# A transformer trunk's opening stage rearranged: transfers in stages behind X, five parts' modulation as column-tiled products, seven product chains side by side and the eighth at the end

## The chip, the cores and the metric

The kernel runs on one core of one Trainium2 chip. TensorE (PE) multiplies matrices into PSUM, VectorE (DVE) and ScalarE (ACT) work on tiles in SBUF and PSUM, GpSimd (POOL) and SyncE (SP) mostly issue transfers. The metric is the device time of one execution in microseconds; less is better.

## The reference

Two layers over 256 latent tokens (x) and 256 context tokens (ctx), width 1024. This is cut to what the opening stage computes:

```python
def rms_norm(x, g):
    y = xf * lax.rsqrt(jnp.mean(xf * xf, axis=-1, keepdims=True) + EPS)
    return (y * g).astype(x.dtype)
def modulate(x, g, shift, scale):
    return rms_norm(x, g) * (1 + scale) + shift
def swiglu(h, w13, w2):
    a, b = jnp.split(h @ w13, 2, axis=-1)
    return (jax.nn.silu(a) * b) @ w2
def half_ffn(x, g, shift, scale, gate, w13, w2):
    return x + 0.5 * gate * swiglu(modulate(x, g, shift, scale), w13, w2)
...
    silu_c = jax.nn.silu(c); silu_cc = jax.nn.silu(c_ctx)
    for i in range(DEPTH):                       # DEPTH = 2
        m  = (silu_c @ w_mod[i] + b_mod[i]).reshape(b, 1, N_MOD, d)     # N_MOD = 9
        mc = (silu_cc @ w_mod[i] + b_mod[i]).reshape(1, 1, N_MOD, d)
        cs = half_ffn(cs, norm_g[i, 0], mc[:, :, 0], mc[:, :, 1], mc[:, :, 2], ffn_w13[i, 0], ffn_w2[i, 0])
        x  = half_ffn(x, norm_g[i, 0], m[:, :, 0], m[:, :, 1], m[:, :, 2], ffn_w13[i, 0], ffn_w2[i, 0])
        # then attention + pooling (layer 0) or a gated MLP (layer 1), then a second half_ffn
```

So before the first product of the first `w13`, the kernel needs the reciprocal root of the mean square of x and ctx, and shift and scale of the first modulation, which are products of a vector (SiLU of c, and of c_ctx) with `w_mod`.

## The kernel before

The tokens lie transposed: X is 8 parts (index k) of 128 channels by 512 columns (256 latent, 256 context). A product in full precision is split in three fp32r matmuls by `mm3`: weights and activations are each held as a rounded high part and the rest (`whi`/`wlo` or `sh`/`sl` for weights, AH/AL for activations), made by `split` (a cast on ScalarE, L153, and a subtraction on VectorE, L154). The first feed-forward has 22 tiles f of a pair of outputs; `start` computes the first four (f = 0 to 3, so 8 chains of products in 8 PSUM banks, 8 parts each, 3 matmuls each: 192 products), and `ffn` goes on with f = 4 and takes these four from `started`. `ffn` loads weights with `load_w`.

What `start` does, in order:

- It loads c, the identity, X and a few rows of `w_mod`; c is spread over the partitions (L665 on TensorE, L667 on ScalarE) into `cc`.
- Squares of X (L679) are summed over the partitions by matmuls with ones (L680); root (L681) and reciprocal (L685) give `rb`.
- The modulation comes in two ways. By dot products on VectorE: `use_mod` multiplies a row tile `wm` with `cc` and sums (L80); a part takes two tiles for two streams, so four of these; `finish_mod` adds the bias (L92, `mod`) and forms the scale (L98, `gs`). By rows on TensorE: `by_rows` multiplies c with `wn` tiles (L697, 384 columns for the 3 last parts), copies the two rows out (L701) and turns them with small matmuls (L704). Before, parts 0 to 4 go by dot products and parts 5 to 7 by rows, in one block.
- Eight steps (i) take the parts in `order`. A step splits the part's weights `raw`, forms `xr` = X times rb (L721), `h` by scale and shift in two halves (L724), AH and AL, and then issues its 24 products.

Engines work each in its own queue, strictly in order; a scheduler in the tile framework has set that order when the program was built, except where an instruction is pinned (`tc.keep_in_program_order`). Transfers are issued by SP (waits of one hold up all behind it), and in `run_mods` by GpSimd. Buffers of a name rotate (`bufs`): `sq` has 2, `raw4` 2, `raw` 2, `whi` and `wlo` 3, `wm` 4, PSUM banks 8.

Of the kernel before, what the change touches and what calls it, by code (L numbers as in the profile page):

```python
# [25 lines left out]
NR = 3  # L26
# [9 lines left out]
def trunk(ctx: ExitStack, tc: tile.TileContext, I, out):  # L36
# [47 lines left out]
    def finish_mod(layer, j, n=1, ks=slice(0, NK)):  # L84
# [7 lines left out]
        V.tensor_tensor(out=m, in0=m, in1=b.broadcast_to([P, ns, n, nk]), op=ALU.add)  # L92
# [32 lines left out]
    def load_w(src, n, pin=lambda ins: ins):  # L125
        raw = wpool.tile([P, 2048], F32, name="raw", bufs=2)
        hi = wpool.tile([P, 2048], F32R, name="whi", bufs=3)
        lo = wpool.tile([P, 2048], F32R, name="wlo", bufs=3)
        nc.sync.dma_start(out=raw[:, :n], in_=src)
        for c in (slice(0, n // 2), slice(n // 2, n)):  # L130
            split(hi[:, c], lo[:, c], raw[:, c], pin)
        return hi, lo
# [82 lines left out]
    def ffn(fi, layer, sub, n, mods, after, started=()):  # L215

        defer = n == T
        with tc.tile_pool(name=f"ffn{fi}", bufs=1) as fp:
            HH = fp.tile([P, NH, 2 * T], F32R, name="HH")
            HL = fp.tile([P, NH, 2 * T], F32R, name="HL")  # L220
            for half in range(2):
                hc = half * T if n == T else 0
                for fl in range(NH):
# [3 lines left out]
                    else:  # L227
                        hi, lo = load_w(I["w13"][fi, f], 2048)
# [410 lines left out]
    def start():  # L639
        ng = 4  # L640
        order = (0, 5, 1, 6, 2, 7, 3, 4)
        with tc.tile_pool(name="start", bufs=1) as sp:
            def get_raw(k):
                raw = sp.tile([P, ng, 2 * P], F32, name="raw4", bufs=2)
                nc.sync.dma_start(out=raw, in_=I["w13"][0, 0:ng, :, k * 2 * P:(k + 1) * 2 * P]
                                  .rearrange("f p c -> p f c"))
                return raw

            cT = sp.tile([P, 2, NK], F32, name="cT")
            nc.sync.dma_start(out=cT, in_=I["cT"])  # L650
            nc.sync.dma_start(out=ident, in_=I["ident"])
            wm = {(0, 0): load_mod(0, 0, nc.sync)}
            for k in range(0, NK, 2):
                nc.sync.dma_start(out=X[:, k:k + 2], in_=I["xc"][:, k:k + 2])
            wm[0, 1] = load_mod(0, 1, nc.sync)
            S.activation(out=cT, in_=cT, func=AF.Silu)

            S.activation(out=rb[:, 0:1], in_=cT[:, 0, 0:1], func=AF.Sqrt, scale=0.0, bias=epsb)

            for st in range(2):  # L660
                for h in range(2):
                    ps = bank()
                    for k4 in range(4):
                        k = 4 * h + k4
                        PE.matmul(ps[:, k4 * P:k4 * P + P], cT[:, st, k:k + 1].broadcast_to([P, P]),  # L665
                                  ident, start=True, stop=True)
                    S.copy(cc[:, st, h * 512:h * 512 + 512], ps)  # L667
            nc.sync.dma_start(out=par, in_=I["par"])
            wn = [wpool.tile([P, 2, 2 * NR * P], F32, name=n, bufs=3 if i > 1 else 2)
                  for i, n in enumerate(("raw", "raw", "whi", "wlo"))]  # L670
            for i in range(4):
                nc.sync.dma_start(out=wn[i], in_=I["w_modr"][:, 2 * i:2 * i + 2])
            raws = {0: get_raw(0)}
            wm.update({(1, h): load_mod(0, 2 + h, nc.sync) for h in range(2)})
            raws[order[1]] = get_raw(order[1])
            ps = bank()
            for k in range(NK):
                sq = tmp.tile([P, 2 * T], F32, name="sq", bufs=2)
                S.activation(out=sq, in_=X[:, k], func=AF.Square)  # L679
                PE.matmul(ps, ones, sq, start=k == 0, stop=k == NK - 1)  # L680
            S.activation(out=rb, in_=ps, func=AF.Sqrt, scale=1.0 / D, bias=epsb)  # L681
            for h in range(2):
                use_mod(0, h, wm[0, h])
            finish_mod(0, 0, 2, slice(0, 1))
            V.reciprocal(rb, rb)  # L685
            sh = sp.tile([P, NK, ng - 2, 2 * P], F32R, name="sh")
            sl = sp.tile([P, NK, ng - 2, 2 * P], F32R, name="sl")
            wh, wl = ([wpool.tile([P, NK, 2 * P], F32R, name=n, bufs=3) for _ in range(2)]
                      for n in ("whi", "wlo"))

            def by_rows():

                row = sp.tile([2, 2 * NR * P], F32, name="row")
                ps = [bank() for _ in range(2)]
                for k in range(NK):
                    for j in range(2):
                        PE.matmul(ps[j][0:2, :NR * P], cT[:, :, k],  # L697
                                  wn[k // 2][:, k % 2, j * NR * P:(j + 1) * NR * P],
                                  start=k == 0, stop=k == NK - 1)
                for j in range(2):  # L700
                    S.copy(row[:, j * NR * P:(j + 1) * NR * P], ps[j][0:2, :NR * P])  # L701
                ps = bank()
                for i in range(2 * NR):
                    PE.matmul(ps[:, 2 * i:2 * i + 2], row[:, i * P:i * P + P], ident[0:2, 0:2],  # L704
                              start=True, stop=True)
                for st in range(2):
                    V.tensor_copy(mod[:, st, :16].rearrange("p (j k) -> p j k", j=2)[:, :, NK - NR:],
                                  ps[:, 0:4 * NR].rearrange("p (j k s) -> p s j k", j=2, k=NR)[:, st])
                finish_mod(0, 0, 2, slice(NK - NR, NK))

            by_rows()
# [127 lines left out]
```

## Time and profile before

| | |
|---|---|
| median of 3 runs | 1141.98 us (1141.77 to 1142.43) |
| profiled execution | 1142.17 us, of which the span of instructions is 1140.4 us |
| TensorE busy | 1132.2 us (99%) |
| VectorE, ScalarE busy | 863.6 us (76%), 522.0 us (46%) |
| transfers | 242.72 MB, mean 213 GB/s |
| granted TensorE clock | 1.000 |

A profile names a group of instructions by line, engine, operation and tiles (output<-inputs). Matmuls overlap: a record's duration holds the time until its result stands, and the distance between starts is the rate. An fp32 matmul leaves two records, an fp32r one leaves one. Span times count from the first instruction.

### The profile page before, as it was taken

The page shows a single profiled execution, that of the slowest core. Times are in us where ns is not written, and L with a number is a line of the kernel's source. Part 1 is how long each engine was busy: PE and PEld are TensorE (multiplying, and loading weights), DVE is VectorE, ACT ScalarE, POOL GpSimd, SP SyncE. Part 2 cuts the span into 40 slices and gives each one's busy share as a digit, 9 for nine tenths or more (in the row PEclk, how much of TensorE's full clock was granted, in tenths as well). Part 3 has the DMA queues.
Part 4 walks back from the last instruction along what each step waited for, and adds up shares of the span by engine and source line. Part 5 has one row for each costly group of instructions (what it writes and reads, how often), then busy time and mean ns, then how long its engine had stood idle before and what let it go on. Part 6 is the DMA issues. An engine that isn't in the chain of part 4 may idle for free.

```text
span 1140.4 us, 19165 instructions
## 1 busy us (share of the span) xinstructions
PE 1132.2 (99%) x7696; PEld 1033.9 (91%) x7696; DVE 863.6 (76%) x1582; ACT 522.0 (46%) x816; POOL 68.4 (6%) x140
## 2 busy tenths in 40 slices
PE   8999999999999999999999999999999999999998
PEld 4888888888888897899999999999999899999998
DVE  5967787878789979777778887656667788756663
ACT  5552212223223357664335456435445866434442
POOL 0000111122222200000000000000000000000000
PEclk9999999999999999999999999999999999999999
DMA  8844656788888850556687566456447536546543
GB/s 323 310 148 156 197 186 234 279 282 325 294 297 306 305 196 11 222 172 223 212 305 264 187 219 218 161 167 219 174 143 257 185 114 219 176 154 237 178 143 114
DMA packets 52408, 242.72 MB, mean 213 GB/s; under 512 B 5600, under 2 KB 11488, under 8 KB 38880
## 3 DMA queue, kind: packets, MB, share of 16 engines
q1 hardware_dynamic: 33888, 174.39, 43.4%
q0 software_dynamic: 18432, 67.12, 17.4%
q8 instruction: 60, 0.98, 0.4%
q14 instruction: 28, 0.23, 0.1%
HBM read 240.44 MB, written 1.05 MB: 212 GB/s over the span
## 4 chain that ended last, share of the span: by engine, by line
PE 97%; DVE 1%; ACT 1%; DMA 1%; issue 0%; SPq 0%; DVEq 0%; ACTq 0%
PE ps L148 30%; PE ps L149 30%; PE ps L150 30%; PE ps L697 1%; PE ps L618 1%; PE ps L619 1%; PE ps L617 1%; PE ps L680 1%; PE ps L665 1%; DMA raw<-in_w_out_a 0%; ACT whi L153 0%; PE ps L501 0%; PE ps L469 0%; DVE st L473 0%; PE ps L172 0%; ACT pe L477 0%
## 5 line engine op out<-in xcount | busy, mean ns | idle before, releaser
L148 PE MATMUL ps<-AH,wlo 128*128 128x258 f32 (+2 forms) x1664 | 507.1, 305 | 0.3 <-ACT AH L153 0.3
L149 PE MATMUL ps<-AH,whi 128*128 128x258 f32 (+2 forms) x1664 | 506.6, 305 | 0.0
L150 PE MATMUL ps<-AL,whi 128*128 128x258 f32 (+2 forms) x1664 | 505.5, 305 | 0.0
L153 ACT CAST whi<-raw 128x1024 fp32r<-128x1024 f32 (+2 forms) x354 | 313.7, 921 | 363.7 <-PE ps L150 260.3
L154 DVE TENSOR_TENSOR wlo<-raw,whi 128x1024 fp32r<-128x1024 f32 (+2 forms) x354 | 367.6, 1064 | 54.4 <-ACT whi L153 53.4
L148 PEld LDWEIGHTS ps<-AH,wlo 128*128 128x128 f32 x1664 | 316.3, 190 | 16.1 <-issue 1.1
L149 PEld LDWEIGHTS ps<-AH,whi 128*128 128x128 f32 x1664 | 314.3, 189 | 14.7 <-issue 0.5
L150 PEld LDWEIGHTS ps<-AL,whi 128*128 128x128 f32 x1664 | 313.4, 189 | 14.5 <-issue 0.2
L150 PE MATMUL ps<-HL,whi 128*128 128x256 f32 (+1 forms) x704 | 218.0, 310 | 0.0
L149 PE MATMUL ps<-HH,whi 128*128 128x256 f32 (+1 forms) x704 | 218.0, 310 | 0.0
L148 PE MATMUL ps<-HH,wlo 128*128 128x256 f32 (+1 forms) x704 | 218.0, 310 | 0.0
L80 DVE CUSTOM_DVE_ANT_0 wm<-wm,cc 128x1024 f32<-128x1024 f32 x138 | 164.7, 1219 | 6.1 <-DMA wm<-in_w_mod 5.0
L148 PEld LDWEIGHTS ps<-HH,wlo 128*128 128x128 f32 x704 | 132.5, 188 | 7.8
L150 PEld LDWEIGHTS ps<-HL,whi 128*128 128x128 f32 x704 | 132.5, 188 | 7.7
L149 PEld LDWEIGHTS ps<-HH,whi 128*128 128x128 f32 x704 | 132.6, 188 | 7.7
L72 POOL DMA_DIRECT2D wm<-in_w_mod x128 | 67.7, 529 | 546.2 <-DVE mod L80 508.6
L206 ACT ACTIVATE sa<-sa,cb 128x256 f32<-128x256 f32 x66 | 33.6, 510 | 119.7 <-DVE sa L205 116.4
L246 DVE SCALAR_TENSOR_TENSOR X<-ps,gate,X 128x256 f32<-128x256 f32 x64 | 30.9, 482 | 48.0 <-PE ps L150 47.9
L204 DVE COPY cb<-ps 128x1 f32<-128x1 f32 x66 | 10.3, 155 | 72.8 <-PE ps L150 72.7
L212 DVE TENSOR_TENSOR h<-ps,sa 128x512 f32<-128x512 f32 x22 | 15.2, 692 | 43.4 <-PE ps L150 34.2
L80 DVE CUSTOM_DVE_ANT_0 junk<-wm,cc 128x1024 bf16<-128x1024 f32 x34 | 41.4, 1218 | 8.6 <-ACT cc L667 7.2
L154 DVE TENSOR_TENSOR HL<-h,HH 128x256 fp32r<-128x256 f32 (+1 forms) x88 | 42.3, 485 | 0.0
(162 smaller groups left out, 705.3 us busy)
## 6 DMA issues: line engine op xcount, KB each, us to landing
raw<-in_w SPq DMA_DIRECT2D x84, 1024.0 KB, 4.9
wm<-in_w_mod POOLq DMA_DIRECT2D x128, 512.0 KB, 5.0
raw<-in_w SPq DMA_DIRECT2D x64, 704.0 KB, 4.1
wm<-in_w_mod SPq DMA_DIRECT2D x10, 512.0 KB, 6.4
raw<-in_w_in_a SPq DMA_DIRECT2D x5, 1024.0 KB, 7.8
raw<-in_w SPq DMA_DIRECT2D x8, 512.0 KB, 5.3
raw<-in_w_out_a SPq DMA_DIRECT2D x4, 1024.0 KB, 5.0
raw<-in_w_in_cu SPq DMA_DIRECT2D x4, 1024.0 KB, 4.8
```

Source lines behind the costliest of these rows:

```text
L72: eng.dma_start(out=w, in_=I["w_mod"][layer, i])
L80: pin(V.tensor_tensor_reduce(out=res, in0=w, in1=cc[:, st, :], scale=1.0, scalar=0.0, op0=ALU.mult, op1=ALU.add, accum_out=mod[:, 2 * laye ...
L148: PE.matmul(ps, wl, xh, start=first, stop=False)
L149: PE.matmul(ps, wh, xh, start=False, stop=False)
L150: PE.matmul(ps, wh, xl, start=False, stop=last)
L153: S.copy(hi, src)
L154: pin(V.tensor_tensor(out=lo, in0=src, in1=hi.bitcast(F32), op=ALU.subtract))
L206: S.activation(out=sa[:, :T], in_=sa[:, :T], func=AF.Silu, bias=cb[:, 0:1])
L212: V.tensor_tensor(out=h32[:, :n], in0=ps[1][:, :n], in1=sa[:, :n], op=ALU.mult)
L246: V.scalar_tensor_tensor(out=X[:, m, :T], in0=ps[:, :T], scalar=gate[:, 2 * layer, sub, m:m + 1], in1=X[:, m, :T], op0=ALU.mult, op1=ALU.add)
L617: PE.matmul(ps[b], AL[:, k, ts], hi[:, ws], start=(k == 0), stop=False)
L618: PE.matmul(ps[b], AH[:, k, ts], hi[:, ws], start=False, stop=False)
```

## The change

- **Transfers.** SP issues c with a selector (`cs`), the identity, X in five pieces, par, the rows of part 3 and the weights of part 3. The rows and weights of part 4, two `wm` tiles and the weights of part 0 are issued by ScalarE's queue (`late`), behind the root. All of these are pinned; the first tiles' weights in `ffn` are pinned too. `raw4` has three buffers.
- **Broadcast of c.** VectorE forms diagonal blocks of the identity times c, and four matmuls with ones spread them; VectorE copies them to `cc`.
- **Sums.** Squares of parts 0 to 5 are added in pairs on VectorE before the matmul with ones; parts 6 and 7 go alone. Three filler matmuls (`warm`) stand between them.
- **Rows.** Parts 3 to 7 now go by rows, one part at a time, 8 matmuls each with 32 columns of weights (c in `c32`, zeros beside it), placed in four column groups of 32; then one copy and two turns with the selector, which also adds the four groups. Part 3's row product stands before the stage; those of parts 4, 5, 6, 7 stand between products of the step before their own. Parts 0, 1, 2 go by dot products, placed in steps 2, 3 and 5 (`jobs`, i = 1, 2, 4).
- **Chains.** Seven chains take each part as it comes, in the order 3, 4, 0, 5, 1, 6, 2, 7; the eighth (f = 3, second output) runs over all parts at the end. The first step runs in two halves of 256 columns, and its AH is written directly.

The diff, cut to its core:

```diff
-    def load_w(src, n, pin=lambda ins: ins):
+    def load_w(src, n, pin=lambda ins: ins, dma_pin=lambda ins: ins):
...
-        order = (0, 5, 1, 6, 2, 7, 3, 4)
+        order = (3, 4, 0, 5, 1, 6, 2, 7)
+        jobs = {1: 0, 2: 1, 4: 2}
...
-                raw = sp.tile([P, ng, 2 * P], F32, name="raw4", bufs=2)
+                raw = sp.tile([P, ng, 2 * P], F32, name="raw4", bufs=3)
...
+            sync, late = InOrder(nc.sync), InOrder(S)
+            sync.dma_start(out=cs, in_=I["cs"])
+            sync.dma_start(out=ident, in_=I["ident"])
+            for ks in (slice(0, 2), slice(2, 4), slice(4, 6), slice(6, 7), slice(7, 8)):
+                sync.dma_start(out=X[:, ks], in_=I["xc"][:, ks])
+            sync.dma_start(out=par, in_=I["par"])
+            get_rows(3)
+            raws[3] = get_raw(3)
...
             for st in range(2):
+                V.tensor_tensor(out=diag[:, st], in0=ident.unsqueeze(1).broadcast_to([P, NK, P]),
+                                in1=c32[:, :, st:st + 1].broadcast_to([P, NK, P]), op=ALU.mult)
                 for h in range(2):
-                    ps = bank()
-                    for k4 in range(4):
-                        k = 4 * h + k4
-                        PE.matmul(ps[:, k4 * P:k4 * P + P], cT[:, st, k:k + 1].broadcast_to([P, P]),
-                                  ident, start=True, stop=True)
-                    S.copy(cc[:, st, h * 512:h * 512 + 512], ps)
+                    PE.matmul(bc[2 * st + h], ones, diag[:, st, 4 * h:4 * h + 4],
+                              start=True, stop=True)
...
                 S.activation(out=sq, in_=X[:, k], func=AF.Square)
-                PE.matmul(ps, ones, sq, start=k == 0, stop=k == NK - 1)
+                if k in (0, 2, 4):
+                    even = sq
+                    continue
+                if k < 6:
+                    V.tensor_tensor(out=sq, in0=even, in1=sq, op=ALU.add)
+                PE.matmul(ps, ones, sq, start=k == 1, stop=k == NK - 1)
+                if k < 6:
+                    warm(1, rw)
...
+            get_rows(4, eng=late)
+            raws[4] = get_raw(4, late)
+            wm.update({(0, j): load_mod(0, j, late) for j in range(2)})
+            raws[0] = get_raw(0, late)
...
+            def by_rows(k):
+                w = rows.pop(k)
+                for kt in range(NK):
+                    g = kt % 4
+                    pin(PE.matmul(rw[32 * g:32 * g + 32, :2 * P], c32[:, kt], w[:, kt],
+                                  start=kt < 4, stop=kt >= 4))
+                row = sp.tile([P, 2 * P], F32, name="row", bufs=2)
+                pin(S.copy(row, rw[:, :2 * P]))
+                for j in range(2):
+                    PE.matmul(rw[:, 2 * P + 2 * j:2 * P + 2 * j + 2], row[:, j * P:j * P + P], sel,
+                              start=True, stop=True)
+                finish_mod(0, 0, 2, slice(k, k + 1), ...)
...
+            by_rows(order[0])
+            warm(4, ps)
-            pss = [[bank(), bank()] for _ in range(ng)]
+            pss = [[bank() for _ in range(2 if f < ng - 1 else 1)] for f in range(ng)]
...
+                if i == 0:
+                    for ts in halves:
+                        if ts.start:
+                            pin(V.reciprocal(rb[:, ts], rb[:, ts]))
+                            subs(pin)
+                            rest(halves[0])
+                        pin(V.tensor_tensor(out=xr[:, ts], in0=X[:, k, ts], in1=rb[:, ts], op=ALU.mult))
+                        if ts.start == 0:
+                            casts(pin)
+                        normed(ts, AH[:, k, ts])
+                        normed(ts, h[:, ts])
+                    rest(halves[1])
...
+                if i in jobs:
+                    d = jobs[i]
+                    for j in range(2):
+                        use_mod(0, 2 * d + j, wm.pop((d, j)), tc.keep_in_program_order)
+                    finish_mod(0, 0, 2, slice(d, d + 1))
...
+                else:
+                    for f, ab in todo:
+                        if ahead is not None and (f, ab) == (1, 0):
+                            by_rows(ahead)
+                        mm3(pss[f][ab], *tile(f, ab), AH[:, k, :2 * T], AL[:, k, :2 * T], False,
+                            i == NK - 1)
+            ps = bank()
+            for k in range(NK):
+                mm3(ps, *tile(ng - 1, 1, k), AH[:, k, :2 * T], AL[:, k, :2 * T], k == 0, k == NK - 1)
```

Three places in the queues as built. TensorE's queue at the front, before (sums L680, row products L697, turns L704, first products):

```order
L665 MATMUL ps<-ident,cT 128x128 x16
L680 MATMUL ps<-sq,ones 128x512 x8
L697 MATMUL ps<-raw,cT 2x384 x8
L697 MATMUL ps<-whi,cT 2x384 x4
L697 MATMUL ps<-wlo,cT 2x384 x4
L704 MATMUL ps<-ident,row 128x2 x3
L148 MATMUL ps<-AH,sl 128x512
```

And now, from the last sums to the second half of the first step (L713 sums, L736 row products, L741 turns, L703 fillers, L832 products of 256 columns):

```order
L713 MATMUL ps<-sq,ones 128x512 x2
L736 MATMUL ps<-raw,c_99 32x256 x8
L741 MATMUL ps<-cs,row 128x2 x2
L703 MATMUL ps<-X,ones 128x256 x4
L832 MATMUL ps<-AH,sh 128x256 x4
L832 MATMUL ps<-AH,whi 128x256 x3
L832 MATMUL ps<-AL,sh 128x256 x4
L832 MATMUL ps<-AL,whi 128x256 x3
L832 MATMUL ps<-AH,sl 128x256 x4
L832 MATMUL ps<-AH,wlo 128x256 x3
L736 MATMUL ps<-raw,c_99 32x256 x8
L832 MATMUL ps<-AH,sh 128x256 x4
```

One row product of 8 narrow matmuls stands where 16 stood, and the next one stands between the two halves of the first step.

ScalarE's queue behind the last square, before (L681 the root, L724 h, L153 casts, L701 the copy of the rows):

```order
L681 ACTIVATE rb<-ps,epsb 128x512 [waits PE_49]
L724 ACTIVATE h_227<-sa,mod,gs 128x256 [waits DVE_49]
L724 ACTIVATE h_227<-sa,mod,gs 128x256
L153 CAST AH<-h_227 128x512 [waits Activation_49]
L153 CAST sh<-raw_131 128x512 [waits DMAHW5_49]
L153 CAST whi<-raw_131 128x256 x2
L701 COPY row<-ps 2x384 [waits PE_49] x2
```

And now (L720 the root in halves, L667 transfers, L739 the copy of part 3's row, L767 casts of its weights, L775 AH and h):

```order
L720 ACTIVATE rb<-ps,epsb 128x256 [waits PE_49]
L720 ACTIVATE rb<-ps,epsb 128x256
L667 DMA raw<-in_w_modr 128x2048
L667 DMA raw_150<-in_w 128x4x256
L667 DMA wm<-in_w_mod 128x1024 x2
L667 DMA raw_156<-in_w 128x4x256
L739 COPY row<-ps 128x256 [waits PE_49]
L767 CAST sh<-raw_97 128x512 [waits DMAHW1_49]
L767 CAST whi<-raw_97 128x256 x2
L775 ACTIVATE AH<-sa,mod,gs 128x256 [waits DVE_49]
```

Five transfers stand between the root and the copy of the first row.

VectorE's queue in the stage, before (L80 dot products, with buffer numbers), around the second step:

```order
L80 ISA junk_234,mod_76<-wm_135,cc_68 128x1024
L80 ISA mod_76 128x1
L92 TENSOR_TENSOR mod_76<-mod_76,par_69 128x2x2x3
L154 TENSOR_TENSOR sl_175<-raw4_137,sh_174 128x512
L98 SCALAR_TENSOR_TENSOR gs_77<-mod_76,par_69 128x2x3
L80 ISA wm_135,mod_76<-wm_135,cc_68 128x1024
L80 ISA mod_76 128x1
L154 TENSOR_TENSOR wlo_178<-raw4_137,whi_176 128x256
L92 TENSOR_TENSOR mod_76<-mod_76,par_69 128x2x2
```

And now, from part 4's AL (second step) to part 0's scale (third step; L81 dot products, L93 and L100 as L92 and L98):

```order
L156 TENSOR_TENSOR AL_73<-h32_273,AH_72 128x512
L81 ISA junk_288,mod_76<-wm_152,cc_68 128x1024
L81 ISA mod_76 128x1
L81 ISA wm_152,mod_76<-wm_152,cc_68 128x1024
L81 ISA mod_76 128x1
L81 ISA junk_291,mod_76<-wm_154,cc_68 128x1024
L81 ISA mod_76 128x1
L81 ISA wm_154,mod_76<-wm_154,cc_68 128x1024
L81 ISA mod_76 128x1
L93 TENSOR_TENSOR mod_76<-mod_76,par_69 128x2x2
L100 SCALAR_TENSOR_TENSOR gs_77<-mod_76,par_69 128x2
```

Part 0's four dot products stand between the second step's last operation and the third step's scale.

176 lines of the change are left out of this document (100 added, 76 removed).

## Prediction

> **What bounds the kernel now.** I read the page first (busy shares, the chain that ended last), then TensorE's waits, then the timeline of the first 30 us engine by engine, then stretches of the opening stage.
>
> ```profile
> span 1140.4 us, 19165 instructions
> PE 1132.2 (99%) x7696; PEld 1033.9 (91%) x7696; DVE 863.6 (76%) x1582; ACT 522.0 (46%) x816; POOL 68.4 (6%) x140
> ...
> PE 97%; DVE 1%; ACT 1%; DMA 1%; issue 0%; SPq 0%; DVEq 0%; ACTq 0%
> ```
>
> TensorE is 97% of the chain that ended last. Its waits are short, and the largest is the very first:
>
> ```profile
> PE ps L665 <- DMA ident<-in_ident: 3.3, 1, 3.3
> PE ps L501 <- ACT pt L493: 0.9, 2, 0.5
> ```
>
> So the end moves only if TensorE gets less work, or waits. The work that is not products of the model sits at the front:
>
> ```profile
> 3.31 6.15 PE L665 MATMUL ps<-ident,cT 128*128 128x128 f32 x32 [3.31 <-DMA ident<-in_ident]
> 9.30 7.42 PE L680 MATMUL ps<-sq,ones 128*128 128x512 f32 x16
> 16.65 5.32 PE L697 MATMUL ps<-raw,cT 128*2 128x384 f32 x16
> ...
> 27.06 0.82 PE L704 MATMUL ps<-ident,row 2*128 2x2 f32 x6
> 27.82 0.50 PE L148 MATMUL ps<-AH,sl 128*128 128x512 f32 x1
> ...
> 28.71 0.82 PE L704 MATMUL ps<-ident,row 2*128 2x2 f32 x6
> ...
> 34.42 0.40 PE L148 MATMUL ps<-AH,sl 128*128 128x512 f32 x1
> 67.76 0.39 PE L148 MATMUL ps<-AH,sl 128*128 128x512 f32 x1
> ```
>
> Columns are start, duration. The first of the 192 opening products starts at 27.82. Steps 2 and 8 of the stage begin at 34.42 and 67.76; 144 products lie between, so one takes 33.34/144 = 0.2315 us and a step of 24 takes 5.56. The stage therefore ends at 67.76 + 5.56 = 73.3. Inside it TensorE never stops, though VectorE is full as well:
>
> ```profile
> 34.00:64.00 30.00, 30.00 (x131) 24.35 (x130) 30.00 (x61) 18.49 (x36) 2.24 (x4) 1.00 0.83 281
> ```
>
> (length, TensorE busy, weight loads, then VectorE's 30.00 and ScalarE's 18.49.) The question is thus one number: when the changed kernel has done the same 192 products, against 73.3. What follows the stage is the same work.
>
> **Prices.** The 16 row products of 384 columns (L697) fill 16.65 to 27.06, 0.65 each; by columns, a plain fp32 matmul of 512 takes 0.87 and one of 256 takes 0.43. Two records make one such matmul. The other prices:
>
> ```profile
> L679 ACT ACTIVATE sq<-X 128x512 f32<-128x512 f32 x8 | 4.9, 628 | 2.3 <-PE ps L680 1.7 <-DMA X<-in_xc 0.6
> L154 DVE TENSOR_TENSOR AL<-h,AH 128x512 fp32r<-128x512 f32 x8 | 5.5, 687 | 0.0
> L154 DVE TENSOR_TENSOR wlo<-raw,whi 128x256 fp32r<-128x256 f32 x16 | 6.3, 418 | 0.0
> L154 DVE TENSOR_TENSOR wlo<-raw,whi 128x1024 fp32r<-128x1024 f32 x3 | 3.6, 1219 | 0.1
> L153 ACT CAST AH<-h 128x512 fp32r<-128x512 f32 x8 | 5.0, 620 | 0.2
> L153 ACT CAST whi<-raw 128x1024 fp32r<-128x1024 f32 x3 | 3.1, 1038 | 0.0
> L724 ACT ACTIVATE h<-sa,mod,gs 128x256 f32<-128x256 f32 x16 | 8.9, 595 | 9.4 <-DVE sa L721 6.8 <-DVE gs L98 2.4
> L685 DVE RECIPROCAL rb<-rb 128x512 f32<-128x512 f32 x1 | 3.4, 3352 | 1.8 <-ACT rb L681 1.8
> L701 ACT COPY row<-ps 2x384 f32<-2x384 f32 x2 | 0.9, 468 | 2.2 <-PE ps L697 2.2
> ```
>
> ```profile
> 16.76 0.69 ACT L681 ACTIVATE rb<-ps,epsb 128x512 f32<-128x512 f32 x1 [1.22 <-PE ps L680]
> ```
>
> ```profile
> 25.25 1.22 DVE L80 CUSTOM_DVE_ANT_0 junk<-wm,cc 128x1024 bf16<-128x1024 f32 x1
> ...
> 26.51 1.23 DVE L80 CUSTOM_DVE_ANT_0 wm<-wm,cc 128x1024 f32<-128x1024 f32 x1
> ...
> 30.86 0.17 DVE L92 TENSOR_TENSOR mod<-mod,par 128x12 f32<-128x12 f32 x1
> ...
> 31.55 0.16 DVE L98 SCALAR_TENSOR_TENSOR gs<-mod,par 128x6 f32<-128x6 f32 x1
> ```
>
> A dot product on VectorE (L80) costs 1.25 with its read-out, and a part by dot products takes four, 5.0.
>
> **Part one: up to the first product.** The broadcast of c becomes four matmuls of 512 behind a VectorE product of 128x1024 (1.22, as L154 at that size). With the identity there at 3.31, TensorE starts at 4.53. It starts slowly:
>
> ```profile
> 3.50:8.00 4.50, 4.50 (x22) 1.00 0.96 350
> 8.40:9.20 0.80, 0.80 (x10) 1.00 0.97 348
> ```
>
> The same L665 records come every 0.21 us until about 8.2 and every 0.1 after, although the granted clock (1.00) reads full in both; full speed came 4.9 us after the first matmul. Taking the same 4.9 here, it comes at 9.4: 2.45 of the 3.48 us of broadcast are done by then, and they end at 10.45. (Bounds: full speed at 8.2 gives 9.8; none before they end gives 11.5.)
>
> Then the sums of squares. They are one matmul for a pair, but only two sq buffers remain, so the second square of a pair waits for TensorE to have read the pair before: matmul 0.87 and some 0.16 until its result stands (a product's record is 0.39 long at 0.2315 apart), square 0.63, addition 0.69, handoffs 0.1, in all 2.45 a round. Two rounds bring the third pair to 15.35; it, a filler and the last two sums (0.87 + 0.43 + 0.87 + 0.87 + 0.16) end at 18.55. Before, the root started at 16.76: what is removed here in matmuls is lost to a ring of waits. The root of one half (0.6) ends at 19.2 and its reciprocal (half of 3.35) at 20.9.
>
> ScalarE now issues five transfers between the roots and the copy of the first row. Such an issue stands on SP alone:
>
> ```profile
> 2.11 1.91 SPq L654 DMA_DIRECT2D X<-in_xc  x4
> ```
>
> 0.48 each, so 2.4 from about 19.0 to 21.4. (Bounds: nothing, if the queue runs on; the row copy is then ready at 19.6, and the reciprocal sets the pace, 1.6 earlier.) The copy of part 3's row, behind them, ends at 21.9, two transposes (of three in 0.82) at 22.45, mod and gs (0.17 + 0.16 and handoffs) at 22.9, the half xr (0.35) at 23.25, AH (0.60) at 23.9. Four filler matmuls (1.73) behind the transposes end at 24.1. The first product starts at 24.1, 3.7 us before 27.82.
>
> **Part two: row products inside the stage.** Before, all 10.4 us of L697 and one block of transposes lay ahead of 27.82, one block after. Now the rows of parts 4 to 7 run between products. Concurrency of column groups shows in the attention:
>
> ```profile
> 446.77 1.09 PE L492 MATMUL ps<-ident,sa 128*128 128x128 f32 x8
> 447.80 0.65 PE L501 MATMUL ps<-pt,VV 128*64 128x256 f32 x2
> 448.81 1.73 PE L501 MATMUL ps<-pt,VV 128*64 128x256 f32 x13 [0.37 <-ACT pt L493]
> ```
>
> Thirteen records of 256 columns in 1.73, the last 0.38 long: 0.1125 apart, where whole-width ones take 0.215. Two groups of 64 columns overlap almost fully. Four groups of 32 I take as four at once: 16 records by 0.054, 0.86, with some 0.1 for each change of mode (the first L501 starts 0.2 behind the last L492 record where 0.11 is usual), 1.05. Ends: pairs only, 1.9; none, 3.5. The Trainium skill, "TensorEngine Tiling (Array Packing)", Theoretical Speedup, allows up to four times for 32 columns, and "TensorE: Matmul & The Clock Gate", Part 3, gives 2.38 times measured for three column tiles; by that efficiency (an estimate) four would take about 1.1 instead of 0.86, and the sum would be 0.9 longer. L501's 1.9 of 2 stands nearer to full overlap. With two transposes (0.45), each row product costs 1.5 on TensorE, four 6.0.
>
> The first step in halves is 42 products of 256: 0.12 each, as
>
> ```profile
> 500.00:550.00 50.00, 50.00 (x416) 1.00 0.58 200
> ```
>
> (all of 258 columns) shows, 5.05 against 4.85: +0.2. The eighth chain is moved, not added.
>
> **Part three: the new waits.** In the queues as they now stand:
> - Step 1, first half: VectorE does xr, the other half's reciprocal (1.68), three subtractions (1.3 pipelined) and only then AL: 26.6. TensorE has finished its seven AH products at 24.95: wait 1.65. The half ends at 28.3, row product 29.35, second half and transposes 32.35.
> - Step 2 (part 4): row copy 30.0, transposes 30.5, gs 30.9, two h (1.09), AH (0.62), 32.7: wait 0.35. It lasts 21 x 0.2315 = 4.86, to 37.55.
> - Step 3 (part 0): four dot products stand behind part 4's AL (33.4): 38.4, gs 38.8, h 39.9, AH 40.55. Wait 3.0. This is the largest.
> - Step 4 (part 5): step 3 with a row product ends at 46.9, but part 5's gs stands behind four more dot products (from 41.2): gs 46.5, h and AH 48.35. Wait 1.5.
> - Steps 5 to 8: VectorE has two dot-product parts behind it and stays ahead. No wait. The weights of the next tile (two casts of 1.04, subtraction 1.22) fit behind the eighth chain's 5.56.
>
> Together 6.5. Dropping two of five dot-product parts from VectorE costs or gains nothing beyond this: it hides wherever it is ahead.
>
> Transfers: the queue moved 366 to 434 GB/s at 7 to 19 us,
>
> ```profile
> GB/s 0 0 15 149 262 355 399 366 295 366 333 333 415 410 410 409 425 434 426 426 418 434 426 426 410 376 360 382 386 415 408 355 321 79 0 165 352 324 355 273
> ```
>
> (slices of 0.75 us) so X, par, part 3's rows and weights (3.9 MB) land by 15, ahead of 19. The queue then lies empty until ScalarE issues at 19; its 3.1 MB are in by about 29, each piece ahead of its use. SP is held in order: its next issue, part 5's weights, waits for part 3's subtractions (26.2) and with the rows behind it lands by about 35, used from 42 on. I cost all that at nothing; what covers it is that TensorE is busy with earlier steps, and a piece 2 us late at step 2 would cost 2. GpSimd's loads start with the next tile, as before.
>
> The other edits have one answer: the earlier table load and the packed c end before the identity lands at 3.31; the pinned transfers of the first tiles only fix an order that the queue has anyway; part 6's and 7's squares as single sums are in the chain above. All cost nothing.
>
> **Sum.** 24.1 + 192 x 0.2315 (44.45) + 0.2 + 6.0 + 6.5 = 81.25, against 73.3: +7.9. The profiled execution took 1142.17; 1150.1, or 1149.9 against the median 1141.98. Its own bounds: ScalarE's issues free (-1.6), early full speed (-0.6), row products at 1.3 (-0.8); late full speed (+1.0), skill's tiling (+0.9): 1146.9 to 1151.8.
>
> **Rivals.**
> - *Preparation stays ahead* (not slower). Place: VectorE's queue in steps 1 to 4. For it: the stage before ran with VectorE full and TensorE without a wait, and 8 of 20 dot products go. The waits of 6.5 vanish, leaving +1.4, 1143.4, within 0.2% (2.3 us, about what a measurement here tells from no change). It decides once the waits together fall under 0.9. Against: before, preparation had until 27.82 to run ahead; now the first product follows part 3's modulation at once, and part 0's comes behind part 4's on the same queue. With it and ScalarE's issues free, it would even be somewhat faster.
> - *Column groups overlap only in pairs*: 1.9 for 1.05 inside the stage, four times +0.9: 1153.5. Not at all: +2.5 each, 1159.9. For it: no row shows more than two.
> - *TensorE slows again in the gaps.* The opening has waits of 2.5 (19.4 to 21.9) and 3.0 at step 3, and the record shows a half-rate start. Each would bring up to 4.9 us at half rate, 2.4 lost, of which the first hides mostly in the wait for AL (0.8 left): +3.2, 1153.1. Against: a gap as long stands nowhere behind the start. "TensorE: Matmul & The Clock Gate", HAM oscillation, in the Trainium skill puts the fall at idle gaps over about 3.4 us; these are just under, and no run here shows one.
>
> **Numbers.** Forecast 0.68; preparation ahead 0.12 (0.08 within 0.2%, 0.04 faster); pairs 0.08, no overlap 0.03; slowing 0.07; 0.02 left for a late transfer. Slower 0.88, same 0.08, faster 0.04. Range 1146 to 1154: forecast's bounds and the pairs and slowing cases, 0.83.
>
> **What would show it.** First product near 24; TensorE idle some 2.5 ahead of it by ScalarE; root at 18.6; row products near 1 us; TensorE waits on AL (1.65) in step 1 and on AH (3.0, 1.5) at steps 3 and 4; first product of the next tile near 81. Wrong if the sums are not held by the sq ring, if steps 3 and 4 start without a wait, or if row products take 2 or more.

## The result, and the profile after

The changed kernel takes 1151.36 us (median of 4 runs, 1150.23 to 1153.16), the kernel before 1141.88 (1141.59 to 1142.43): a ratio of 1.0084, 95% interval 1.0066 to 1.0101. It is 9.5 us slower; 1149.9 was forecast, in a range of 1146 to 1154. The profiled execution took 1150.23, at a mean granted clock of 0.998; the kernel before has 1.000.

The page's first lines, and TensorE's waits in the first 95 us:

```profile
span 1148.5 us, 19290 instructions
PE 1130.8 (98%) x7757; PEld 1034.2 (90%) x7757; DVE 863.3 (75%) x1581; ACT 520.5 (45%) x818; POOL 68.4 (6%) x140
```

```profile
PE ps L694 <- DVE cc L691: 4.5, 1, 4.5
PE ps L150 <- ACT AH L155: 4.1, 3, 2.6
PE ps L741 <- ACT row L739: 2.1, 1, 2.1
PE ps L713 <- DVE sq L712: 2.0, 2, 1.0
```

TensorE's busy time is 1.4 us less than before, and yet the span is 8.1 longer. In that time TensorE waited 3.3 before, for the identity; now the list adds up to 12.7. Its timeline shows where (start, duration; the wait ahead in brackets):

```profile
4.55 5.21 PE L694 MATMUL ps<-cc,ones 128*128 128x512 f32 x8 [4.55 <-DVE cc L691]
9.60 1.02 PE L713 MATMUL ps<-sq,ones 128*128 128x512 f32 x2
12.07 1.13 PE L713 MATMUL ps<-sq,ones 128*128 128x512 f32 x2 [1.01 <-DVE sq L712]
14.64 1.12 PE L713 MATMUL ps<-sq,ones 128*128 128x512 f32 x2 [1.01 <-DVE sq L712]
17.84 1.07 PE L736 MATMUL ps<-raw,c 128*32 128x256 f32 x16
21.03 0.81 PE L741 MATMUL ps<-cs,row 128*128 128x2 f32 x4 [2.12 <-ACT row L739]
21.70 3.45 PE L703 MATMUL ps<-X,ones 128*128 128x256 f32 x8
24.80 0.83 PE L832 MATMUL ps<-AH,sh 128*128 128x256 f32 x4
...
27.75 1.07 PE L736 MATMUL ps<-raw,c 128*32 128x256 f32 x16
28.75 0.74 PE L832 MATMUL ps<-AH,sh 128*128 128x256 f32 x4
...
32.23 0.50 PE L150 MATMUL ps<-AH,sl 128*128 128x512 f32 x1 [0.18 <-ACT AH L155]
...
39.95 0.50 PE L150 MATMUL ps<-AH,sl 128*128 128x512 f32 x1 [2.61 <-ACT AH L155]
...
48.09 0.50 PE L150 MATMUL ps<-AH,sl 128*128 128x512 f32 x1 [1.35 <-ACT AH L155]
...
81.38 0.40 PE L150 MATMUL ps<-AH,wlo 128*128 128x512 f32 x1
```

The first product starts at 24.80 (27.82 before). The last row is the first product of the next tile: 81.38. By the same count the kernel before has it at 73.30:

```profile
73.30 0.40 PE L148 MATMUL ps<-AH,wlo 128*128 128x512 f32 x1
```

So 3.0 us are won ahead of the stage and 11.1 lost inside it: 8.1, the whole difference of the two profiled executions. One thing is new: the four fillers (L703) behind the transposes take 3.45 where eight such records should take 1.73. By stretches (start and end, length, TensorE busy; the granted clock is the third column from the end):

```profile
17.87:21.28 3.41, 1.29 (x20) 0.64 (x19) 1.75 (x1) 1.51 (x4) 0.00 (x0) 1.00 0.61 202
21.28:24.70 3.42, 3.42 (x11) 2.88 (x11) 2.73 (x5) 1.91 (x5) 0.00 (x0) 0.50 1.01 389
24.70:28.10 3.40, 3.40 (x31) 3.00 (x34) 2.84 (x8) 1.10 (x2) 0.00 (x0) 1.00 1.04 371
```

For 3.42 us, right behind the wait of 2.12, TensorE ran at half its clock.

### The profile page after: what moved, and what is told of

It is laid out like the page before. It is cut to its first block, busy times and chain, and to the rows that moved or that the text cites. A ratio compares the mean times of both kernels' runs of the same rounds, so it can differ in the third digit from the quotient of the medians.

```text
span 1148.5 us, 19290 instructions
## 1 busy us (share of the span) xinstructions
PE 1130.8 (98%) x7757; PEld 1034.2 (90%) x7757; DVE 863.3 (75%) x1581; ACT 520.5 (45%) x818; POOL 68.4 (6%) x140
## 3 DMA queue, kind: packets, MB, share of 16 engines
HBM read 240.44 MB, written 1.05 MB: 210 GB/s over the span
## 4 chain that ended last, share of the span: by engine, by line
PE 95%; DVE 2%; ACT 2%; DMA 1%; issue 0%; ACTq 0%; SPq 0%; DVEq 0%
PE ps L150 30%; PE ps L152 30%; PE ps L151 30%; PE ps L620 1%; PE ps L621 1%; PE ps L622 1%; PE ps L694 0%; DMA raw<-in_w_out_a 0%; PE ps L713 0%; ACT whi L155 0%; PE ps L736 0%; PE ps L504 0%; PE ps L472 0%; PE ps L703 0%; DVE st L476 0%
## 5 line engine op out<-in xcount | busy, mean ns | idle before, releaser
L150 PE MATMUL ps<-AH,wlo 128*128 128x258 f32 (+2 forms) x1661 | 505.8, 305 | 0.3 <-ACT AH L155 0.3
L151 PE MATMUL ps<-AH,whi 128*128 128x258 f32 (+2 forms) x1661 | 505.4, 305 | 0.0
L155 ACT CAST whi<-raw 128x1024 fp32r<-128x1024 f32 (+1 forms) x338 | 307.9, 945 | 365.4 <-PE ps L152 254.8
L156 DVE TENSOR_TENSOR wlo<-raw,whi 128x1024 fp32r<-128x1024 f32 (+1 forms) x338 | 361.5, 1095 | 64.3 <-ACT whi L155 63.5
L150 PEld LDWEIGHTS ps<-AH,wlo 128*128 128x128 f32 x1661 | 315.7, 190 | 16.0 <-issue 1.1
L151 PEld LDWEIGHTS ps<-AH,whi 128*128 128x128 f32 x1661 | 313.7, 189 | 14.6 <-issue 0.5
L151 PE MATMUL ps<-HH,whi 128*128 128x256 f32 (+1 forms) x704 | 218.0, 310 | 0.0
L150 PE MATMUL ps<-HH,wlo 128*128 128x256 f32 (+1 forms) x704 | 218.0, 310 | 0.0
L81 DVE CUSTOM_DVE_ANT_0 wm<-wm,cc 128x1024 f32<-128x1024 f32 x134 | 160.2, 1220 | 9.5 <-DMA wm<-in_w_mod 8.9
L151 PEld LDWEIGHTS ps<-HH,whi 128*128 128x128 f32 x704 | 132.6, 188 | 7.7
L150 PEld LDWEIGHTS ps<-HH,wlo 128*128 128x128 f32 x704 | 132.5, 188 | 7.7
L206 DVE COPY cb<-ps 128x1 f32<-128x1 f32 x66 | 10.3, 155 | 70.8 <-PE ps L152 70.7
L155 ACT CAST HH<-h 128x256 fp32r<-128x256 f32 (+1 forms) x88 | 39.7, 454 | 2.7 <-DVE h L214 2.3
```

The costliest lines, as they stand in the source:

```text
L81: pin(V.tensor_tensor_reduce(out=res, in0=w, in1=cc[:, st, :], scale=1.0, scalar=0.0, op0=ALU.mult, op1=ALU.add, accum_out=mod[:, 2 * laye ...
L150: PE.matmul(ps, wl, xh, start=first, stop=False)
L151: PE.matmul(ps, wh, xh, start=False, stop=False)
L155: S.copy(hi, src)
L156: pin(V.tensor_tensor(out=lo, in0=src, in1=hi.bitcast(F32), op=ALU.subtract))
```

## The experiments

Times are medians; "again" is the changed kernel beside the first group, 1150.59.

| run | median us | to the kernel before (95%) |
|---|---|---|
| again | 1150.59 | 1.0081 (1.0067 to 1.0095) |
| late_on_sync | 1150.93 | 1.0077 (1.0064 to 1.0089) |
| no_part0_dots | 1146.47 | 1.0042 (1.0029 to 1.0055) |
| squares_no_ring | 1149.04 | 1.0062 (1.0050 to 1.0075) |
| one_column_group | 1162.31 | 1.0169 (1.0155 to 1.0183) |
| fill_start_gap | 1151.24 | 1.0079 (1.0065 to 1.0093) |
| fill_step3_gap | 1148.69 | 1.0054 (1.0041 to 1.0066) |
| no_inner_rows | 1144.02 | 1.0014 (1.0006 to 1.0023) |
| early_rows | 1139.41 | 0.9976 (0.9966 to 0.9986) |
| early_rows_warm | 1141.92 | 0.9999 (0.9990 to 1.0007) |

The runs were taken in three groups, and the kernel before, run beside each, took 1142.09, 1142.30 and 1142.28. These differ by 0.2, so a difference between kernels of two groups that is well above 0.2 is not the groups'. A trace is of one execution, whose time can lie 1 us off the median.

**again.** No edit.

> The changed kernel once more, as the baseline of the other runs of this group. Its first four runs stood at 1150.2, 1150.3, 1152.4 and 1153.2, with mean granted clocks of 0.998, 0.998, 0.996 and 0.995; the profiled one (0.998) has one half-rate stretch of 3.4 us, at 21.3 to 24.7. Theory: the two levels are a second half-rate stretch, whose 1.7 us no wait hides; then the times again fall near 1150.3 or 2 to 3 above it, and each 0.001 of mean clock goes with some 1.1 us. Rival: the spread is the chip's own; then the kernel before shows the same spread in this group.

Four runs fell at 1150.35 to 1150.77 (clock 0.998), one at 1153.13 (0.995); the kernel before stayed at 1.000 and within 1.7 us. With the first four runs that makes three of nine that are 2 to 3 us longer at 0.995 or 0.996. That the lower clock goes with the time is shown; where its extra half-rate time lies is not, since no run of that level has a trace.

**no_part0_dots.** The waits at steps 3 and 4.

```
+V.memset(mod, 0.0)
...
 for j in range(2):
-    use_mod(0, 2 * d + j, ...)
+    if d:
+        use_mod(0, 2 * d + j, ...)
```

> The four dot products for part 0's modulation are left out (its modulation is then the bias alone); everything else stands. Theory (the waits at steps 3 and 4, 2.61 and 1.35, are VectorE's queue behind these four dot products): both waits vanish, 4.0 less, 1146.2 where the changed kernel gives 1150.2. Rival: VectorE or ScalarE is full anyway, and the wait comes back at steps 4 to 6: a gain of 1 to 2.6. Rival: part 5's row or weights are the late ones at step 4: only the 2.6 goes.

4.1 us less: as the theory said. Its trace has neither wait; of TensorE's waits for AH only step 2's is left (L151 here is L150 above):

```profile
PE ps L151 <- ACT AH L156: 0.5, 1, 0.5
```

So VectorE's queue was the whole of both waits: part 0's four dot products hold step 3, and part 1's four, which then begin late, hold step 4 (without part 0's they begin at 37.11 instead of 40.54). No wait came back at later steps, so VectorE was not full. The traced execution, at 1147.56 one of the slower ones, ran at half rate for 6.8 us behind the first gap (21.28 to 28.11) and starts step 2 at 34.04 instead of 32.23; even so it is 2.8 less than the traced execution of "again".

**no_inner_rows.** The largest term of the forecast, taken away.

```
-for kt in range(NK):
+for kt in range(NK if k == order[0] else 0):
...
-for j in range(2):
+for j in range(2 if k == order[0] else 0):
```

> The four row products inside the stage and their transposes are left out of TensorE (parts 4 to 7 take part 3's modulation row); the transfers, row copies, casts and all else stand. Theory (each costs TensorE some 1.7 on the path: 1.0 of products, 0.4 of transposes and 0.3 of changes between them): steps 1, 6 and 8's share of it goes, 5.1 in all, while step 3's 1.7 only lengthens the wait at step 4, which hangs on dot products: 1145.5 where the changed kernel gives 1150.5; with a half-rate stretch at step 3 in the open, 1147. Rival: preparation on VectorE and ScalarE is the bound in steps 5 to 8 too, and waits take the place of the row products: 1148 to 1150.

6.6 us less, 1.5 more than expected. The rival is out: waits did not take the place of the row products. What was expected wrongly is the wait at step 4 (second row; the first is step 3's):

```profile
38.40 0.50 PE L150 MATMUL ps<-AH,sl 128*128 128x512 f32 x1 [1.71 <-ACT AH L155]
44.54 0.50 PE L150 MATMUL ps<-AH,sl 128*128 128x512 f32 x1 [1.00 <-ACT AH L155]
```

It did not grow by 1.7 but shrank from 1.35 to 1.00. VectorE's queue shows why. With the row products gone, the scheduler set part 5's scale (L100) behind three of part 1's dot products, where the changed kernel has it behind all four; and the dot products themselves begin 1.55 earlier (38.99 for 40.54), since part 4's modulation no longer waits for its transposes. The scale in the changed kernel, then here:

```profile
45.59 0.16 DVE L100 SCALAR_TENSOR_TENSOR gs<-mod,par 128x2 f32<-128x2 f32 x1
```

```profile
42.55 0.16 DVE L100 SCALAR_TENSOR_TENSOR gs<-mod,par 128x2 f32<-128x2 f32 x1
```

It stands 3.0 earlier, and ScalarE no longer forms a half of the next part's h ahead of AH; AH starts 3.6 earlier (43.87 for 47.43), while step 3 ends 3.2 earlier. So this run changes the order on VectorE too, and 6.6 is not the price of the row products alone.

**one_column_group.** What the column tiling is worth.

```
-g = kt % 4
+g = 0
...
-    start=kt < 4, stop=kt >= 4))
+    start=kt == 0, stop=kt == NK - 1))
```

> The row products' eight matmuls all write the first group of 32 columns, one after the other; the other three groups' rows keep what an earlier filler left there, so the modulation of parts 3 to 7 is not the reference's. Theory (the four groups run side by side: 16 records in 1.0 us here): without that the records come some 0.11 apart, a row product takes 1.75 to 1.85 instead of 1.0, and the three inside steps that are not followed by a wait pay 0.8 each, 2.4 more (the one in step 3 is taken up by the wait of 1.35 at step 4): 1152.8 where the changed kernel gives 1150.5. Rival: the groups only hide each other's loads of weights, and the single group costs 1.2 at most: within 0.7 of the changed kernel.

```profile
29.72 3.64 PE L736 MATMUL ps<-raw,c 128*32 128x256 f32 x16
33.29 0.74 PE L832 MATMUL ps<-AH,sh 128*128 128x256 f32 x4
```

A row product takes 3.57 in one group (29.72 to 33.29) and 1.00 in four (27.75 to 28.75): 3.6 times. Both theories were far off, through my error: 0.11 is the spacing of two groups side by side; alone, a record of 256 columns takes 0.22, and the prediction's own "none, 3.5" was the right figure. The kernel is 11.7 us slower; four times 2.57, for the row products inside the stage, are 10.3 of that, and the rest is not separated.

**squares_no_ring.** The ring of two sq buffers.

```
-sq = tmp.tile(..., name="sq", bufs=2)
+sq = tmp.tile(..., name=("sq", "sa", "h32", "sq")[k // 2], bufs=2)
```

> The eight squares take turns in three pairs of buffers (two of them are idle at that time) instead of one pair. Theory (a ring of two sq buffers holds the sums at 2.57 a round): squares follow X's landings, TensorE's two waits of 1.0 vanish, the sums end near 15.2 instead of 17.83 and all behind them moves by 2.6: 1147.6 where the changed kernel gives 1150.2. If the half-rate stretch behind the hold by ScalarE comes from how much TensorE idled before it, it gets shorter or goes; if it comes from the 2.1 us gap alone, it stays. Rival: the sums are held by X's transfers or the broadcasts of c: they end after 17 and the gain is under 0.8. Rival: part 4's rows and weights, issued 2.6 earlier, land no earlier: half of the gain is lost in step 2.

Sums and first half moved as expected: part 4's row product starts at 24.99 where "again" has 27.97. But only 1.55 of the 2.6 arrived. The half-rate stretch had gone from behind the first gap, though that gap is still 2.10, and stood behind the wait of step 3, where nothing hides it:

```profile
37.19 0.50 PE L150 MATMUL ps<-AH,sl 128*128 128x512 f32 x1 [2.62 <-ACT AH L155]
...
39.10 1.94 PE L736 MATMUL ps<-whi,c 128*32 128x256 f32 x16
```

```profile
34.93:38.34 3.41, 1.15 (x5) 0.97 (x6) 3.34 (x10) 1.71 (x3) 0.00 (x0) 1.00 0.38 142
38.34:41.75 3.41, 3.41 (x21) 1.39 (x20) 3.04 (x6) 0.64 (x2) 0.66 (x1) 0.50 0.91 323
```

From step 3's first product to step 4's it is 9.68 here and 8.16 in "again": 1.5 lost.

**late_on_sync.** ScalarE's five issues.

```
-sync, late = InOrder(nc.sync), InOrder(S)
+sync = late = InOrder(nc.sync)
```

> The five late transfers (part 4's rows and weights, the first two of part 0's modulation tiles, part 0's weights) are issued on SyncE behind part 3's weights, no longer on ScalarE. Theory (ScalarE's issues hold the first row copy): the copy starts near 19.0 instead of 20.60, TensorE's idle time ahead of the transposes falls from 2.1 to under 0.6, the granted clock stays at full, the first product comes near 21.7 instead of 24.80, the AL wait of step 1 returns (1.4) and the first half ends some 2 us earlier: 2 us less, 1148.2 where the changed kernel gives 1150.2. Rival: the reciprocal and the AL behind the subtractions set the pace anyway: 1149.5 to 1150.2. Rival: transfers that are issued earlier slow X or the rows; then the sums end after 17.9 and the time is that of the changed kernel or above.

The wait ahead of the transposes fell to 0.49 and the AL wait came back (1.40), both as expected; the time did not fall. From the first sum to part 4's row product it takes 16.31 (10.84 to 27.15), 2.0 less than the 18.33 of "again", so in this trace the rival that something else sets the pace does not hold. Two things of the clock ate the gain. The broadcasts took 6.42 instead of 5.21, so that everything started 1.2 later; the sums end after 17.9 for that reason, not for the transfers, since their rounds are still 2.57. And the stretch came at step 3, which takes 1.5 more than in "again":

```profile
37.41:40.82 3.41, 1.47 (x6) 1.05 (x6) 3.41 (x7) 1.71 (x3) 0.00 (x0) 1.00 0.33 110
40.82:44.23 3.41, 3.41 (x20) 1.75 (x20) 2.72 (x6) 1.20 (x4) 0.66 (x1) 0.50 0.94 337
```

**fill_start_gap.** Work for TensorE in the first gap.

```
+if k == order[0]:
+    warm(5, bc[0])
 row = sp.tile([P, 2 * P], F32, name="row", bufs=2)
```

> Five more filler matmuls stand between the first row products and their transposes, in the 2.1 us in which TensorE waits for ScalarE. Theory (the half-rate stretch from 21.3 comes of that idle time): the granted clock stays full there, the four fillers behind the transposes take 1.73 instead of 3.45, the first product comes with AH near 23.3 instead of 24.80, and TensorE then waits for AL as forecast, some 1.6; the time hardly moves, 1150.3, since the slow stretch lay in that wait's shadow. If the stretch is then found at step 3, as in the run with more buffers for the squares, the time is 1.3 to 1.7 longer. Rival: the stretch has nothing to do with the idle time; it stays at 21 to 25 and the five fillers at half rate make it longer, 1151 or more.

As the theory said: full clock throughout (1.0 in the profiled run), the fillers in 1.97, the AL wait back:

```profile
22.85 1.97 PE L703 MATMUL ps<-X,ones 128*128 128x256 f32 x8
...
27.04 0.75 PE L834 MATMUL ps<-AL,sh 128*128 128x256 f32 x4 [1.40 <-DVE AL L781]
```

The time is 1151.24, no gain (its sums started 1.15 later than those of "again"). So the stretch came of the idle time, and in the changed kernel it lay almost wholly in the shadow of the wait for AL: from the first sum to part 4's row product it is 18.09 here (10.79 to 28.88) and 18.33 in "again" (9.64 to 27.97).

**fill_step3_gap.** squares_no_ring, and work in the gap of step 3.

```
 else:
+    if i == 2:
+        warm(5, rw)
     for f, ab in todo:
```

> The kernel with more buffers for the squares (1149.04) and five useless filler matmuls ahead of step 3's products, in the 2.6 us in which TensorE waits for part 0. Theory (the half-rate stretch of 3.4 us that this kernel showed at 38.3 to 41.8 follows from that idle time): it goes, and more work on TensorE makes the kernel faster by 1.2 to 1.7: 1147.6. Rival: the stretch comes of the low share of work before, or of something else, and stays: the fillers run in idle time, 1149.0, or delay step 3, 1149.5.

```profile
35.69 2.32 PE L703 MATMUL ps<-X,ones 128*128 128x256 f32 x10
38.45 0.49 PE L150 MATMUL ps<-AH,sl 128*128 128x512 f32 x1 [0.44 <-ACT AH L155]
...
46.59 0.50 PE L150 MATMUL ps<-AH,sl 128*128 128x512 f32 x1 [1.36 <-ACT AH L155]
```

The stretch at step 3 is gone: step 4's first product comes 8.14 behind step 3's (38.45 to 46.59) where squares_no_ring needs 9.68 (37.19 to 46.87). Useless work won 1.5 us there. The median is only 0.35 lower: in the traces, this kernel's broadcasts took 6.46 instead of 5.18. A stretch stands behind its first gap again (20.39 to 23.81), hidden by the wait for AL.

**early_rows.** Put together: the buffers of squares_no_ring; all transfers on SyncE in the order of use; and

```
-order = (3, 4, 0, 5, 1, 6, 2, 7)
-jobs = {1: 0, 2: 1, 4: 2}
+order = (3, 4, 5, 0, 6, 1, 7, 2)
+jobs = {1: (0, 0), 2: (0, 1), 3: (1, 0), 4: (1, 1), 5: (2, 0), 6: (2, 1)}
...
-warm(4, ps)
...
 # step 1
+by_rows(4)    # ahead of the first product
+by_rows(5)    # between the AH and the AL products of the first half
```

> A version made from the findings: more buffers for the squares; all transfers on SyncE in the order of use; parts in the order 3, 4, 5, 0, 6, 1, 7, 2; the row products of part 4 in place of the four fillers and those of part 5 in the wait for AL of step 1; the four dot products of a part two by two behind the preparation of two parts. Theory (the loss is the waits behind the dot products, 4.1, the ring, 2.6, ScalarE's issues, 1.9, and row products on the path, 1.7 each, two of them): from 1150.5 in all 4.1 + 2.6 + 1.9 + 3.4 = 12.0 less, 1138.5, under the kernel before by 3.5; no half-rate stretch behind the start, since no idle time above 1 us is left. Rival: VectorE, with 34 us of preparation behind its 24th us, becomes the bound and waits come back at steps 4 to 8: 1140 to 1144. Rival: rows of parts 4 and 5, issued behind part 3's, land after 17 and 20 and hold TensorE's queue ahead of the first product: 1 to 3 longer.

1139.41, 11.2 us less than "again" and 0.24% (0.14 to 0.34) faster than the kernel before. TensorE's waits in its first 95 us:

```profile
PE ps L699 <- DVE cc L696: 4.6, 1, 4.6
PE ps L737 <- DVE mod L93: 1.2, 2, 0.9
PE ps L742 <- ACT row L740: 0.5, 1, 0.5
```

No wait on AH is left and the clock is full throughout; steps 2 to 8 run without a stop, and no wait is for a transfer, so neither rival holds. The theory's 1138.5 is missed by 0.9; in the trace the broadcasts took 6.22, 1.0 more than those of "again".

**early_rows_warm.** early_rows, and

```
+rw = bank()
+for _ in range(8):
+    PE.matmul(rw[:, :P], ones, ones, start=True, stop=True)
```

> The version with early rows and eight small matmuls of the tile of ones on itself from 1.1 on, while the identity is on its way. Theory (TensorE runs at half rate until 3 to 6 us after its first matmul, so the broadcasts of c last 5.2 to 6.4 for 3.5): full rate comes by 7, the sums end some 2 earlier, and the order of the queue, which the scheduler changes with it, leaves 0.5 to 2.0: 1137.4 to 1138.9 where the version without them gave 1139.4. Rival: the sums are then held by X's last transfer and the squares behind it, or the rows of parts 4 and 5 land too late: no change, 1139.4. Rival: the half rate at the start has a fixed end, whatever TensorE does: no change either, and the broadcasts' records show it.

```profile
1.09 3.78 PE L695 MATMUL ps<-ones 128*128 128x128 f32 x16 [1.09 <-DVE ones L65]
4.66 4.50 PE L702 MATMUL ps<-cc,ones 128*128 128x512 f32 x8
```

The broadcasts took 4.50 instead of 6.22, and the row product of part 3 starts at 14.68 instead of 16.34: the start of the clock is no fixed time. But the kernel became slower, 1141.92, its runs spread over 5 us at clocks of 0.993 to 1.000. The scheduler had put part 4's row product behind five of the first products; TensorE then waits 1.5 for AH and 0.9 for AL, and a half-rate stretch of 6.8 follows (23.5 to 30.3 in the profiled run). None of my cases had that. Its two runs at 1.000 took 1140.04 and 1140.70, so even those show no gain over early_rows.

## Why the prediction was right

Its mechanism held: the time won ahead of the stage is less than what the row products inside it and the waits behind the dot products cost. That the sum came within 0.13 of the profiled stage end (81.25 against 81.38) is luck, since its terms err against each other:

- **First product, 24.1: measured 24.80.** Full rate came 3.1 us behind the first matmul, by the trace's record of the clock at 7.63, and not 4.9: 1.54 of the 3.48 of broadcasts were done by then, which makes 9.57, and the sums started at 9.60, not 10.45. The ring was right: rounds of 2.57 (2.45), sums ended at 17.91 (18.55). ScalarE's five issues held the row copy, 2.6 in all:

```profile
17.96 0.38 ACTq L667 DMA_DIRECT2D raw<-in_w_modr  x1
18.38 0.44 ACTq L667 DMA_DIRECT2D raw<-in_w  x1
18.85 1.22 ACTq L667 DMA_DIRECT2D wm<-in_w_mod  x2
20.10 0.46 ACTq L667 DMA_DIRECT2D raw<-in_w  x1
20.60 0.37 ACT L739 COPY row<-ps 128x256 f32<-128x256 f32 x1 [1.82 <-issue]
```

  The fillers, counted at 1.73, took 3.4 at half rate and set the first product.
- **AL in step 1, 1.65: measured 0.** It stood behind those fillers; in the runs with full clock there it is 1.40.
- **Steps 2, 3 and 4, 0.35, 3.0 and 1.5: measured 0.18, 2.61 and 1.35,** and by no_part0_dots the last two are what was said, VectorE's queue behind the dot products of part 0 and then of part 1. All waits together: 4.1 for 6.5, the largest error, 2.4.
- **Row products, 4 x 1.5: measured 1.00 for the products as against 1.05, but about 1.7 with all.** Step 3 lasts from 39.95 to 46.74 (48.09 less its wait), 6.79 for 21 products of 0.2315, 4.86; step 2, which has no row product, runs 0.25 over its 4.86. That leaves 1.7. The 1.05 was to hold the changes between the products and the groups; the 1.00 is without them, and they add some 0.1 each, as does the first product behind the transposes. The four come to 6.7; taking them out gave 6.6, with shorter waits and a longer slow stretch in the same run.
- **Halves, +0.2: measured +0.9** (2.95 and 2.85, without the transposes, for 42 products of 0.1157, 4.86): the starts of the groups of four on a new operand, as it seems (0.58 where four products of 0.1157 make 0.46). The slow stretch has no part in it: the runs at full clock there need 3.0 for the first half, less their wait for AL.
- **Transfers, nothing: measured nothing.** No wait of TensorE in the list is put down to one, and between 18 and 50 us none of ScalarE or VectorE. The prediction's row of slices shows 333 to 434 GB/s at 7 to 19 us, not 366 to 434; nothing hung on it.

In sum 0.7 + 0.7 + 0.7 too little, 2.4 too much, and the 0.4 that is left I put to small starts behind waits.

The rivals: *preparation stays ahead* fails on the two waits. *Pairs* and *no overlap* fail on 1.00 against 3.57. *TensorE slows in the gaps* was a case of its own at 0.07, and half of it came true: it did slow behind the first gap, at next to no cost, as its text said, and in the profiled execution not behind that of step 3. "TensorE: Matmul & The Clock Gate" of the Trainium skill (HAM oscillation) puts the fall at idle gaps over about 3.4 us, and on that ground I gave gaps of 2.5 and 3.0 a small chance to matter. The trace disagrees: 2.12 was enough. That the median of the four runs lies 1.1 above the profiled time goes with the two runs at clocks of 0.995 and 0.996; with the five runs of "again" it is 1150.59.

## What to carry to other kernels

Work that is moved into the stream of an engine that is always busy costs its full price there unless a wait takes it up: the four row products cost some 6.7 us inside, while the time ahead of the first product shrank by 3.0 only. Look first for the waits which the stream still has, and put the moved work there. early_rows did that with two of the four, counted at 3.4 of the 12.0 that it was to win; the rest was counted on the waits, the ring and ScalarE's issues, and the run does not part them. And treat a gap of 2 us on TensorE as more than 2 us: it can be followed by a stretch at half clock, 1.5 us lost where nothing hid it, which shows in the granted clock of the profile and in no list of waits.

## What the runs showed of the hardware

- **Where the clock changes.** Each trace holds a record of the granted clock. In all twelve traces the changes lie whole multiples of 3.413 us apart; in the changed kernel full rate begins at 7.63, falls to half at 21.29, four times 3.413 later, and is back at 24.70. I cut the first 79 us of every trace into windows at these edges. Nine traces have a fall to half rate there. In eight of them TensorE had been busy 1.04 to 1.47 of the 3.41 us ahead of it, and a window with 1.56 or more was followed by a fall only once. So it counts where a gap lies, not its length alone. The changed kernel's gap of 2.12 lies within one window (17.87 to 21.28, busy 1.29, shown above). The 2.61 ahead of step 3 is cut by an edge, and no fall follows:

```profile
34.92:38.33 3.41, 2.43 (x11) 1.67 (x9) 3.31 (x9) 0.17 (x1) 0.00 (x0) 1.00 1.01 378
38.33:41.74 3.41, 1.79 (x10) 1.21 (x14) 3.41 (x7) 1.54 (x3) 0.00 (x0) 1.00 0.40 138
```

  In squares_no_ring it is the other way round: the first gap, 2.10, is cut and not followed by a fall, and the 2.62 ahead of step 3 lies almost wholly in one window (34.93 to 38.34, busy 1.15), with a fall behind it.

```profile
14.45:17.87 3.42, 1.93 (x19) 0.51 (x17) 1.75 (x1) 0.84 (x2) 0.00 (x0) 1.00 0.34 98
17.87:21.28 3.41, 2.81 (x17) 2.60 (x18) 2.07 (x4) 2.59 (x6) 0.00 (x0) 1.00 1.02 396
```

  Part 1 (The HAM clock gate) of "TensorE: Matmul & The Clock Gate" in the Trainium skill has a free-running window of 3413 ns, which the lengths agree with. Two things stay open. early_rows_warm does not fit a mere share of busy time: 2.49 of 3.41 went ahead of its stretch, a part of it in row products of 32 columns. And in three traces the half rate lasted two windows, though TensorE was busy all through the first.
- **The start.** Ahead of the first entry in that record the granted clock reads 1.00, though matmuls come at twice their spacing: in the kernel before every 0.21 us until about 8.2 and every 0.1 after, and its record begins at 8.23. Full rate begins at 7.63 to 7.67 in five traces and at 9.70 to 10.15 in four, with the first matmul at 4.55 to 4.75 in all nine. In the five, an edge lies at about 4.2 and TensorE is busy 2.90 to 3.08 of the window behind it; in the four, the first matmul falls into the middle of a window, busy 1.69 to 2.17, and full rate comes one window later. That is why the broadcasts took 5.1 to 5.2 us in some kernels and 6.2 to 6.5 in others. What sets the place of the edges is not shown, so a difference of 1 us between two of these kernels can be that alone.
- **Column groups.** Four groups of 32 columns in fp32: 16 records in 1.00 us against 3.57 in one group.
